# A two-block transformer on one core: order of the second block's steps around the change from grouped-query to neighbourhood attention

## Chip, cores and metric

One core of a Trainium2 chip runs the whole program. The metric is device microseconds of one execution. Three runs of the kernel before took 1642.47, 1636.21 and 1642.05 us, median 1642.05 us.

## The reference, cut to what matters

The program computes two blocks on 512 tokens of width 1024. The change lies in the second, which puts 16 meta tokens ahead of the 512 and runs two layers of this form:

```python
h = rms_norm_2(x, norm_g)
qa, ka, va, za, qb, kb, vb, zb, ga, gb = split_cols(einsum('bld,de->ble', h, w_in))
oa = gqa_attention(rope(norm(qa)), rope(norm(ka)), va) * silu(za)     # 8 heads, 2 groups
ob = neighbourhood_attention(qb, kb, vb, rpb) * silu(zb)              # 8 heads, 8x16 window and the meta keys
mixed = sigmoid(ga) * (oa @ w_o_attn) + sigmoid(gb) * (ob @ w_o_na)
return x + mixed @ w_out
```

Meta rows are queries too in the first layer; in the second they are keys only. The reference writes no order between the ten projections and the two attentions, as long as each has its inputs.

## The kernel before

Every projection is done with operands split into a high and a low part (fp32r), as three matmuls per product (`mm`, L173 to L175). A weight tile is loaded by SP (L157, 512 KB, pool `wr`, 2 buffers), its high part is cast on ACT (L137, `whi`, 3 buffers), its low part is made on GpSimd (L147, four pieces) or, in `dense` mode, on VectorE (L140).

`b2_attention` runs a layer's attention from a string of steps, `B2_ORDER[li]`. The part before the bar is grouped-query attention, the part behind it neighbourhood attention. The steps are:

- `t` rope tables, `k` keys and values, `q0` and `q1` queries of a group, each with normalisation and rope; the turned queries of `q1` go through `bankD` (L1408).
- `A hd p` scores and exponentials of two blocks of 128 queries (L1477, L1485, L1486), `P hd p` their normalisation, transposes and values (L1498, L1502, L1508, L1514, L1516), `E` the gating of a finished head, `m g` the meta queries of a group (scores L1477 with `qm`).
- `Z br pr` a gate of an attention output (L1449), `G br m` a gate of the mix (L1701): each is one weight tile and 48 matmuls of 264 columns in the first layer, 24 of 512 in the second.
- `Q pr` the neighbourhood queries and keys of two heads: two weight tiles, 96 matmuls of 264 columns in the first layer, splits, and four copies between partitions issued by SP (L1586 for the keys). `V half` the neighbourhood values: two weight tiles, 16 matmuls for the meta rows (L1348) and 96 for four tiles of tokens.
- `S hd p` neighbourhood scores (L1615, L1617, L1618, L1621), `T hd p` their normalisation and transposes (L1634, L1638, L1643), `O hd` values (L1656), `M` the meta queries.

Three facts set what a step can wait for. First, all of `Z`, `G`, `Q`, `V`, `k` and `q` take their accumulators from `bankD`: two banks of `ps_d`, and for every third call, in the order of the string, the one bank of `ps_e`:

```python
        self.nd += 1
        pool = self.ps_e if self.ps_e and self.nd % 3 == 0 else self.ps_d
```

Second, the pool `k` has 4 buffers. The two of grouped-query keys (`kd`, one a group) are free again when the last scores on them are through; each `Q` takes two (`ks`, one a head of the pair). Third, the values of neighbourhood attention (`vb`) take space of the pools `va`, `r`, `rd` and `rope`, so that they can be written only when the last values of grouped-query attention are through.

The string sets the order in which instructions are traced, not the order in which the engines get them: the tile context is opened with `schedule_with_timeline_sim=True`, which arranges each engine's queue by its own estimate of when operands are ready. Of the first steps up to three `Z` or `G` are started early: their first halves are traced one after the other, then their second halves (`early` in `b2_attention`).

Of the kernel before, what the change touches and what calls it, by code (L numbers as in the profile page):

```python
# [40 lines left out]
class Build:  # L41
# [1109 lines left out]


    B2_BANKS = dict(s=2), dict(p=1)
    B2_ORDER = ("Z01 Z00 G11 t k q0 A00 P00 Z03 A30 A01 P01 A10 E00 G03 P10 A11 P11 A20 E01 P20 A21 P21 q1 G00 A31 E02 A41 P30 A40 P31 Z02 E03 A50 A51 P40 A61 P41 E04 Z10 A60 P50 Q0 P51 G01 Q2 E05 m0 A70 A71 P60 P61 E06 G05 P70 P71 E07 G02 m1 Z11 | V0 S00 S10 S01 V1 T00 S11 T10 Q1 T11 T01 S20 O0 T20 S21 E10 O1 S30 E11 S40 S31 T21 S41 T30 O2 T40 Z12 S50 E12 T31 T41 O3 T50 E13 O4 Q3 S51 Z13 G10 S70 S60 E14 T51 G04 O5 S61 T60 E15 M S71 T61 T70 O6 G14 G13 T71 G12 E16 O7 E17", "Z00 Z02 t k q0 A00 P00 A01 P01 A10 E00 A11 P10 G11 P11 A21 A20 E01 G01 Z01 q1 P20 A40 P21 A30 E02 P30 A31 A51 P31 A41 E03 A50 P40 P41 E04 P50 P51 Z03 Z10 A60 A61 E05 Q2 A70 G10 P60 P61 E06 G00 G05 G02 Q0 P70 A71 P71 E07 | S00 V0 T00 Q1 V1 S01 S10 S11 T01 O0 S20 T10 T11 S21 E10 O1 E11 T20 T21 S40 S30 Z11 O2 E12 S31 T30 T31 S41 O3 G04 E13 T40 Z12 T41 S50 O4 T50 Q3 S51 E14 T51 O5 S60 S61 Z13 T60 S70 T61 E15 S71 G12 G14 O6 T70 E16 T71 O7 E17 G03 G13")

    def layer(self, li, h):
        nc, a = self.nc, self.a
# [31 lines left out]
    def b2_attention(self, li, h):  # L1189
# [4 lines left out]
        early = []  # L1194
        for part, pairs, pools in zip(self.B2_ORDER[li].split("|"), (True, False), (("va", "r", "rd", "rope"), ("vb",))):
            with ExitStack() as ctx:
# [636 lines left out]
```

## Time and profile before

| | us |
|---|---|
| median of 3 runs | 1642.05 |
| the profiled execution | 1641.14 |
| its span | 1639.0 |
| PE busy in the span | 1554.7 |
| DVE, ACT, POOL busy | 963.0, 765.0, 508.8 |

In the profiled execution the attention of the first layer lies at about 700 to 1060 us and that of the second at about 1195 to 1510 us. A stretch row gives, for each engine, the busy time and the number of instructions, then the granted TensorE clock, the share of DMA and the GB/s. A timeline row gives start and duration of merged instructions, what they write and read, and in brackets the idle time before them with what ended it.

### The profile page before, as it was taken

How to read it: one execution, taken by the hardware profiler on the slowest of the kernel's cores; microseconds unless marked ns; L12 is line 12 of the kernel's file. 1: busy time of each engine (PE TensorE's matmuls, PEld its weight loads, DVE VectorE, ACT ScalarE, POOL GpSimd, SP SyncE). 2: the span in 40 equal slices, each digit the busy share in tenths (PEclk: the TensorE clock that was granted, in tenths of full speed). 3: DMA queues.
4: the chain of work that ended last, by engine and by line, in shares of the span. 5: the costliest groups of instructions: out<-in, count | busy, mean ns of one | idle time of the engine just before them, and what ended most of it. 6: DMA issues, size and time to landing. Idle time of an engine off the chain costs nothing. (4 is left out here: it accounts for less than half of the span.)

```text
span 1639.0 us, 25892 instructions
## 1 busy us (share of the span) xinstructions
PE 1554.7 (95%) x9694; PEld 1378.3 (84%) x9694; DVE 963.0 (59%) x2156; ACT 765.0 (47%) x1727; POOL 508.8 (31%) x641
## 2 busy tenths in 40 slices
PE   6999999889999999999899999999999997999997
PEld 5788977778888888799898899999798896988785
DVE  4476567745444435658865558545568648665453
ACT  4465566734333323644554446433345455554332
POOL 4663443131111112325432243011455340431022
PEclk9999989989999999999998999999999999999999
DMA  5532222455333333322131134135322330342252
GB/s 163 143 112 69 65 75 82 148 185 169 90 97 96 103 104 116 104 89 78 40 87 54 54 111 131 46 92 180 116 77 78 86 92 18 99 121 88 78 183 73
DMA packets 189376, 163.60 MB, mean 100 GB/s; under 512 B 9664, under 2 KB 161312, under 8 KB 189252
## 3 DMA queue, kind: packets, MB, share of 16 engines
q1 hardware_dynamic: 189252, 161.96, 32.9%
q8 instruction: 76, 1.25, 0.3%
q14 instruction: 48, 0.39, 0.1%
HBM read 139.19 MB, written 12.58 MB: 93 GB/s over the span
## 5 line engine op out<-in xcount | busy, mean ns | idle before, releaser
L147 POOL TENSOR_TENSOR wlo<-wraw,whi 128x256 fp32r<-128x256 f32 (+1 forms) x384 | 284.3, 772 | 370.5 <-ACT whi L137 351.7
L137 ACT CAST whi<-wraw 128x1024 fp32r<-128x1024 f32 (+2 forms) x216 | 212.0, 982 | 327.8 <-PE psd L174 79.6
L173 PE MATMUL psd<-hh,whi 128*128 128x264 f32 (+2 forms) x1016 | 339.7, 335 | 3.9 <-DVE k L202 1.4
L174 PE MATMUL psd<-hl,whi 128*128 128x264 f32 (+2 forms) x1016 | 338.4, 333 | 0.0
L175 PE MATMUL psd<-hh,wlo 128*128 128x264 f32 (+2 forms) x1016 | 337.2, 332 | 0.5 <-DVE wlo L140 0.5
L140 DVE TENSOR_TENSOR wlo<-wraw,whi 128x1024 fp32r<-128x1024 f32 (+1 forms) x119 | 135.9, 1142 | 205.1 <-ACT whi L137 204.9
L173 PEld LDWEIGHTS psd<-hh,whi 128*128 128x128 f32 x1016 | 192.8, 190 | 23.1 <-ACT hh L201 1.6
L175 PEld LDWEIGHTS psd<-hh,wlo 128*128 128x128 f32 x1016 | 192.9, 190 | 18.1 <-DVE wlo L140 1.0
L174 PEld LDWEIGHTS psd<-hl,whi 128*128 128x128 f32 x1016 | 193.2, 190 | 16.9
L173 PE MATMUL psd<-whi,hh 128*128 128x256 f32 (+2 forms) x484 | 138.8, 288 | 4.9 <-ACT mo L371 2.4
L175 PE MATMUL psd<-whi,hl 128*128 128x256 f32 (+2 forms) x484 | 137.8, 285 | 0.0
L174 PE MATMUL psd<-wlo,hh 128*128 128x256 f32 (+2 forms) x484 | 137.4, 285 | 0.0
L173 PEld LDWEIGHTS psd<-whi,hh 128*128 128x128 f32 x484 | 91.5, 190 | 6.1 <-ACT mo L371 2.6
L342 POOL TENSOR_TENSOR y<-x,g 128x512 f32<-128x512 f32 (+1 forms) x34 | 46.9, 1391 | 147.3 <-DVE x L534 103.2
L201 ACT CAST pt<-pst 128x512 fp32r<-128x512 f32 (+3 forms) x130 | 63.9, 505 | 61.1 <-PE pst L1502 49.6
L175 PEld LDWEIGHTS psd<-whi,hl 128*128 128x128 f32 x484 | 91.8, 190 | 0.3
L174 PEld LDWEIGHTS psd<-wlo,hh 128*128 128x128 f32 x484 | 91.6, 190 | 0.4
L202 DVE TENSOR_TENSOR pt<-pst,pt 128x512 fp32r<-128x512 f32 (+3 forms) x130 | 75.1, 583 | 28.2 <-ACT pt L201 27.2
L1143 POOL TENSOR_TENSOR act<-conv,act 128x512 fp32r<-128x512 f32 x16 | 25.4, 1586 | 161.7 <-ACT act L1142 161.7
L1485 DVE TENSOR_REDUCE gls<-pss 128x1 f32<-128x528 f32 (+1 forms) x66 | 46.5, 704 | 38.4 <-PE pss L1477 37.5
L1486 ACT ACTIVATE pr<-pss,gls 128x528 f32<-128x528 f32 (+1 forms) x66 | 46.4, 703 | 35.2 <-DVE gls L1485 33.0
L175 PE MATMUL pss<-oh,wlo 128*128 128x264 f32 (+1 forms) x192 | 61.6, 321 | 0.0
(478 smaller groups left out, 3631.9 us busy)
## 6 DMA issues: line engine op xcount, KB each, us to landing
wraw<-in_w_in_dram SPq DMA_DIRECT2D x108, 512.0 KB
wraw<-in_w_up_dram SPq DMA_DIRECT2D x32, 512.0 KB
wraw<-in_w_out_dram SPq DMA_DIRECT2D x24, 512.0 KB
wraw<-in_w_down_dram SPq DMA_DIRECT2D x16, 512.0 KB
nbias<-in_na_bias_dram SPq DMA_DIRECT2D x16, 408.0 KB
k<-k SPq DMA_DIRECT2D x16, 296.0 KB
wraw<-in_w_ple_gate_dram SPq DMA_DIRECT2D x8, 512.0 KB
wraw<-in_w_o_attn_dram SPq DMA_DIRECT2D x16, 256.0 KB
```

The lines of the kernel that those rows point to most:

```text
L137: nc.scalar.copy(hi, raw)
L140: nc.vector.tensor_sub(lo, raw, hi.bitcast(F32))
L147: nc.gpsimd.tensor_sub(lo[:, p[0], p[1]], raw[:, p[0], p[1]], hi[:, p[0], p[1]].bitcast(F32))
L173: m(ps, A[0], B[0], start=start, stop=False)
L174: m(ps, A[0], B[1], start=False, stop=False)
L175: m(ps, A[1], B[0], start=False, stop=stop)
L201: nc.scalar.copy(hi, src)
L202: nc.vector.tensor_sub(lo, src, hi.bitcast(F32))
L342: self.nc.gpsimd.tensor_tensor(y[:n, c], x[:, c], g[:n, c], op=OP.mult)
L1143: nc.gpsimd.tensor_sub(lo, u, hi.bitcast(F32))
L1485: nc.vector.tensor_reduce(mx, sv, axis=AX.XY, op=OP.max, negate=True)
L1486: nc.scalar.activation(pr.rearrange("p (a n) -> p a n", a=2), sv, AF.Exp, bias=mx, accum_out=l)
```

## The change

The same 237 steps stand in the same four parts (two layers, ahead of the bar and behind it); only their order within a part differs.

First layer, before the bar (old above new):

```
Z01 Z00 G11 t k q0 A00 P00 Z03 A30 A01 P01 A10 E00 G03 P10 A11 P11 A20 E01 P20 A21 P21 q1 G00 A31 E02 A41 P30 A40 P31 Z02 E03 A50 A51 P40 A61 P41 E04 Z10 A60 P50 Q0 P51 G01 Q2 E05 m0 A70 A71 P60 P61 E06 G05 P70 P71 E07 G02 m1 Z11
Z01 Z00 t k q0 A00 P00 Z03 A30 G11 A01 P01 A10 E00 G03 P10 A11 P11 A20 E01 P20 A21 P21 q1 G05 A31 E02 A41 P30 G02 A40 G00 P31 Z02 E03 A50 A51 Z10 P40 A61 P41 E04 A60 P50 Q0 P51 G01 E05 m0 A70 A71 P60 P61 E06 P70 P71 Q2 E07 m1 Z11
```

Behind the bar, the first steps (the rest is as before but for S61, which goes ahead of O5):

```
V0 S00 S10 S01 V1 T00 S11 T10 Q1 T11 T01 S20 O0 T20 S21 E10 O1
V0 Q1 S00 S10 S01 T00 S11 T10 T11 T01 S20 O0 T20 S21 E10 V1 O1
```

Second layer, before the bar:

```
Z00 Z02 t k q0 A00 P00 A01 P01 A10 E00 A11 P10 G11 P11 A21 A20 E01 G01 Z01 q1 P20 A40 P21 A30 E02 P30 A31 A51 P31 A41 E03 A50 P40 P41 E04 P50 P51 Z03 Z10 A60 A61 E05 Q2 A70 G10 P60 P61 E06 G00 G05 G02 Q0 P70 A71 P71 E07
Z00 Z02 t k q0 A00 P00 A01 P01 A10 E00 A11 P10 G11 P11 A20 E01 G01 Z01 q1 A21 P20 A40 P21 A30 E02 P30 A31 A51 P31 A41 E03 A50 P40 Z10 P41 E04 P50 P51 Z03 A60 A61 E05 Q2 A70 G10 P60 P61 E06 G00 Q0 G05 P70 A71 P71 E07 G02
```

Behind its bar T10, S40 and T40 go some places forward, Z13 goes behind T60, and the gates G12 and G13 come forward from the end, to behind T30 and behind E13.

One value differs by the order: in the first layer O0 now precedes V1, whose last instruction copies the meta keys' values to partitions 32 to 47 of `vbm`; head 0 there multiplies the low parts of the meta keys' weights by what stood in those partitions.

## Rows read from the trace of the kernel before

**Rows 1.** Page, busy time of each engine over the span

```profile
PE 1554.7 (95%) x9694; PEld 1378.3 (84%) x9694; DVE 963.0 (59%) x2156; ACT 765.0 (47%) x1727; POOL 508.8 (31%) x641
```

**Rows 2.** Stretches of both layers: PE, PEld, DVE, ACT, POOL, clock, DMA share, GB/s

```profile
700.00:800.00 100.00, 93.81 (x732) 91.12 (x733) 75.70 (x193) 47.96 (x117) 48.34 (x63) 0.95 0.24 73
800.00:870.00 70.00, 70.00 (x587) 69.56 (x586) 47.66 (x100) 39.93 (x91) 22.32 (x36) 1.00 0.26 70
870.00:930.00 60.00, 52.31 (x371) 47.68 (x370) 36.38 (x77) 27.11 (x66) 11.04 (x17) 0.89 0.15 42
930.00:1060.00 130.00, 129.78 (x1103) 128.08 (x1103) 80.28 (x252) 67.59 (x172) 39.91 (x61) 1.00 0.34 99
1343.00:1393.00 50.00, 40.70 (x310) 36.15 (x309) 39.79 (x84) 27.16 (x62) 2.81 (x4) 1.00 0.13 36
```

**Rows 3.** Stretches of 10 us inside them, the same columns

```profile
780.00:790.00 10.00, 8.56 (x67) 7.26 (x66) 9.69 (x26) 7.44 (x17) 4.71 (x6) 1.00 0.01 2
790.00:800.00 10.00, 6.93 (x42) 6.51 (x42) 9.63 (x22) 3.53 (x9) 7.40 (x11) 0.83 0.37 105
...
890.00:900.00 10.00, 7.54 (x34) 6.54 (x33) 5.39 (x12) 2.66 (x9) 0.74 (x2) 0.55 0.15 31
```

**Rows 4.** Timeline of PE, first layer, around the change of attentions

```profile
884.91 0.28 PE L1516 MATMUL pso<-pm,vm 128*128 128x256 f32 x1
...
891.95 0.45 PE L1348 MATMUL psd<-whi,hm 128*48 128x256 f32 x1 [1.94 <-DVE z L1450]
...
913.50 0.73 PE L1477 MATMUL pss<-k,qm 128*64 128x264 f32 x4
...
917.65 0.39 PE L173 MATMUL psd<-hh,whi 128*128 128x264 f32 x1 [0.78 <-DVE k L202]
917.88 0.28 PE L174 MATMUL psd<-hl,whi 128*128 128x264 f32 x1
...
920.42 0.28 PE L174 MATMUL psd<-hl,whi 128*128 128x264 f32 x1
```

**Rows 5.** Timeline of ACT, first layer: key splits and gates

```profile
846.73 0.39 ACT L1701 ACTIVATE sg<-psd 128x264 f32<-128x264 f32 x1 [0.49 <-PE psd L175]
...
890.16 0.64 ACT L201 CAST k<-psd 64x264 fp32r<-64x264 f32 x2
...
914.59 0.65 ACT L201 CAST k<-psd 64x264 fp32r<-64x264 f32 x2
...
923.11 0.37 ACT L1701 ACTIVATE sg<-psd 128x264 f32<-128x264 f32 x1
```

**Rows 6.** Timeline of the SP queue, first layer: the two copies of keys

```profile
893.60 25.52 SPq L1586 DMA_DIRECT2D k<-k  x2
```

**Rows 7.** Timeline of PE, first layer, behind q1

```profile
788.17 0.66 PE L1408 MATMUL psd<-ident,rd 128*128 128x128 f32 x4 [0.84 <-DVE rd L1396]
...
794.49 0.74 PE L1514 MATMUL pso<-pt,va 128*128 128x256 f32 x4 [3.06 <-DVE pt L202]
```

**Rows 8.** Timeline of ACT, second layer: key splits of Q0

```profile
1344.66 0.37 ACT L201 CAST k<-psd 64x264 fp32r<-64x264 f32 x1
...
1383.00 0.65 ACT L201 CAST k<-psd 64x264 fp32r<-64x264 f32 x2
```

**Rows 9.** Page, group of the low parts of weights

```profile
L147 POOL TENSOR_TENSOR wlo<-wraw,whi 128x256 fp32r<-128x256 f32 (+1 forms) x384 | 284.3, 772 | 370.5 <-ACT whi L137 351.7
```

**Rows 10.** Timeline of PE, start of the first layer

```profile
711.47 0.37 PE L173 MATMUL psd<-hh,whi 128*128 128x264 f32 x1
```

**Rows 11.** Timeline of DVE, start of the first layer

```profile
712.37 0.69 DVE L202 TENSOR_TENSOR hl<-pst,hh 128x512 fp32r<-128x512 f32 x1 [0.45 <-ACT hh L201]
```

**Rows 12.** Timeline of ACT, start of the first layer

```profile
717.09 1.05 ACT L137 CAST whi<-wraw 128x1024 fp32r<-128x1024 f32 x1 [2.41 <-PE psd L174]
```

**Rows 13.** Timeline of PE, neighbourhood scores and turns of the first layer

```profile
944.50 0.40 PE L1615 MATMUL pss<-k,q 128*128 128x256 f32 x2
...
955.41 0.60 PE L1638 MATMUL pst<-ident,nsb 128*128 128x128 f32 x4
```

More of the change, by code (lines that the diff above doesn't have):

```diff
@@ L1153 @@
     B2_BANKS = dict(s=2), dict(p=1)
-    B2_ORDER = ("Z01 Z00 G11 t k q0 A00 P00 Z03 A30 A01 P01 A10 E00 G03 P10 A11 P11 A20 E01 P20 A21 P21 q1 G00 A31 E02 A41 P30 A40 P31 Z02 E03 A50 A51 P40 A61 P41 E04 Z10 A60 P50 Q0 P51 G01 Q2 E05 m0 A70 A71 P60 P61 E06 G05 P70 P71 E07 G02 m1 Z11 | V0 S00 S10 S01 V1 T00 S11 T10 Q1 T11 T01 S20 O0 T20 S21 E10 O1 S30 E11 S40 S31 T21 S41 T30 O2 T40 Z12 S50 E12 T31 T41 O3 T50 E13 O4 Q3 S51 Z13 G10 S70 S60 E14 T51 G04 O5 S61 T60 E15 M S71 T61 T70 O6 G14 G13 T71 G12 E16 O7 E17", "Z00 Z02 t k q0 A00 P00 A01 P01 A10 E00 A11 P10 G11 P11 A21 A20 E01 G01 Z01 q1 P20 A40 P21 A30 E02 P30 A31 A51 P31 A41 E03 A50 P40 P41 E04 P50 P51 Z03 Z10 A60 A61 E05 Q2 A70 G10 P60 P61 E06 G00 G05 G02 Q0 P70 A71 P71 E07 | S00 V0 T00 Q1 V1 S01 S10 S11 T01 O0 S20 T10 T11 S21 E10 O1 E11 T20 T21 S40 S30 Z11 O2 E12 S31 T30 T31 S41 O3 G04 E13 T40 Z12 T41 S50 O4 T50 Q3 S51 E14 T51 O5 S60 S61 Z13 T60 S70 T61 E15 S71 G12 G14 O6 T70 E16 T71 O7 E17 G03 G13")
+    B2_ORDER = ("Z01 Z00 t k q0 A00 P00 Z03 A30 G11 A01 P01 A10 E00 G03 P10 A11 P11 A20 E01 P20 A21 P21 q1 G05 A31 E02 A41 P30 G02 A40 G00 P31 Z02 E03 A50 A51 Z10 P40 A61 P41 E04 A60 P50 Q0 P51 G01 E05 m0 A70 A71 P60 P61 E06 P70 P71 Q2 E07 m1 Z11 | V0 Q1 S00 S10 S01 T00 S11 T10 T11 T01 S20 O0 T20 S21 E10 V1 O1 S30 E11 S40 S31 T21 S41 T30 O2 T40 Z12 S50 E12 T31 T41 O3 T50 E13 O4 Q3 S51 Z13 G10 S70 S60 E14 T51 G04 S61 O5 T60 E15 M S71 T61 T70 O6 G14 G13 T71 G12 E16 O7 E17", "Z00 Z02 t k q0 A00 P00 A01 P01 A10 E00 A11 P10 G11 P11 A20 E01 G01 Z01 q1 A21 P20 A40 P21 A30 E02 P30 A31 A51 P31 A41 E03 A50 P40 Z10 P41 E04 P50 P51 Z03 A60 A61 E05 Q2 A70 G10 P60 P61 E06 G00 Q0 G05 P70 A71 P71 E07 G02 | S00 V0 T00 Q1 V1 S01 S10 S11 T10 T01 O0 S40 S20 T11 S21 E10 O1 E11 T20 T21 S30 Z11 O2 E12 S31 T30 G12 T31 T40 S41 O3 G04 E13 G13 Z12 T41 S50 O4 T50 Q3 S51 E14 T51 O5 S60 S61 T60 Z13 S70 T61 E15 S71 G14 O6 T70 E16 T71 O7 E17 G03")
     def layer(self, li, h):
```

## The prediction

> **What bounds the kernel now.** I read the page's busy times first: PE works 1554.7 of 1639.0 us, DVE 963.0 [rows 1]. Moving steps takes no matmul away, so only the 84 us in which PE stands idle, and the time in which it runs slowly, can be won or added to. The stretches then say where this lies in the code that is moved [rows 2]. From 800 to 870 PE is busy for all of the 70.00 us, and in the neighbourhood attention from 930 to 1060 for 129.78 of 130. It is not full in three places: 700 to 800 (idle 6.2 us), 870 to 930 (idle 7.7 us, with a mean clock of 0.89) and 1343 to 1393 (idle 9.3 us, clock 1.00).
>
> The ten-microsecond stretches and the timelines say why. **At the first layer's change** no engine is full: from 890 to 900 DVE is busy 5.39 us, ACT 2.66, and the clock is granted at 0.55, between the two levels of 1.2 and 2.4 GHz, after PE's gap of 1.94 us [rows 3, 4]. What is missing is a place to write. Q2's keys lie in two of the three banks of `bankD`; their split for one head is made at 890.16, for the other only at 914.59, 24.4 us later [rows 5], since that head's buffer is the grouped-query key `kd[1]`, and its last readers are the meta scores of m1 at 913.50 [rows 4]. Only then, at 917.65, released by the split of `k`, does the next half gate begin on PE; its tanh follows at 923.11 [rows 4, 5]. SP stands behind the same wait: its two copies of keys take from 893.60 to 919.12 [rows 6].
>
> **Behind q1** (780 to 800) DVE is busy 9.69 and 9.63 of 10 us [rows 3], and PE waits for the rope of a turn that itself sits in a bank of `bankD` and, for 3.06 us, for a split [rows 7]. I take the stall as 1.4 + 3.1 us idle plus 17% of 6.93 us for the clock of 0.83: 5.7 us. That at 870 to 930 is 7.7 us plus 11% of 52.31 us: 13.5 us.
>
> **In the second layer** all gates have run early, Q0 holds two banks from about 1344.66 until `kd[1]` comes free and the split at 1383.00 can be made [rows 8], and PE gets little but grouped-query work. DVE is busy 39.79 of 50 us there [rows 2].
>
> Two things follow. A gate is not done where it stands in the string: G01 stands behind P51, but its first tanh is through at 846.73 and P51's last matmul only at 884.91 [rows 4, 5], since the build arranges each queue by estimate. And what counts of an order is which work is left when grouped-query attention runs dry, and which banks it finds.
>
> **The change, part by part.** A gate or Z issues one load on SP, one cast on ACT, four GpSimd pieces of 0.77 us [rows 9] and 48 matmuls; 21 starts from 917.88 to 920.42 give 0.121 us each [rows 4], so 5.8 us of PE. Q and V issue two loads, casts and eight pieces, and 11 to 14 us of PE. All of it is issued in both orders; what is moved is the cover.
>
> *Start, first layer.* G11 is no longer the third early step. Its first half runs on PE from 711.47, while the low part of the last token tile is not there before 712.37 + 0.69 = 713.06 [rows 10, 11]: 1.6 us without cover now. Against it, the first key weights find a free `whi` buffer, where their cast at 717.09 had waited 2.41 us for PE to finish with one [rows 12]. Bounds 0 to +2.9 (a whole half); I take **+1.6**. SP passes one load fewer before the rope tables' loads.
>
> *G11 ahead of A01.* Its 5.8 us of PE now lie between q0 and q1, and grouped-query attention starts that much earlier. The stall behind q1 is 5.7 us, of which DVE's share moves forward with the start. But its other half is banks: the turns of q1 keep their three, and G05 behind them takes the place of G00. Bounds -5.7 to 0; I take **-4**.
>
> *G05, G02 and Z10 early, Q2 late.* By the count of `bankD` calls, G02's first half and Z11's second half fell on the banks that Q2's keys held. Now 96 matmuls (11.6 us) come ahead of Q2, so its hold begins later, while m1, which ends it, keeps its place; and behind Q2 only Z11 follows, with one half on a held bank. G02's half (24 x 0.121 = 2.9 us) is then not left over, and with it one `whi` buffer fewer is held, so that the second weights of V0 can be cast and one tile of V0 can run in the stall, another 2.9 us. Of the 13.5 us I take **-5**, by the two halves, less a little since the fillers also run out earlier; bounds -13.5 (the hold is gone) to +3 (one half more is shut in).
>
> *Q1 ahead of S00, V1 behind E10.* Q1 goes past the bias loads in SP's queue, and its eight GpSimd pieces past V1's; GpSimd is busy 39.91 of 130 us there [rows 2]. Its keys need the buffers of heads 0 and 1, whose last scores (S11) now stand behind it, so it holds two banks until then. The trace has no such hold here; its cover is V0 and the first half of Q1, and the scores wait for T00, which before came 10.9 us behind S01 only because V1 was on PE [rows 13]. Bounds 0 to +10 (the hold of 24.4 us at the rate of the first layer's, 13.5 us lost in 60, is 5.5 us; twice that with copies and biases behind it on SP); I take **+1**, nearest to the full stretch of 930 to 1060.
>
> *Second layer.* G02 behind E07 is the only gate left for the dry end; Q0, two gates ahead, takes one bank of each kind, so G05, G02 and one tile of V0 share the third. But V0's meta rows, which had the `ps_e` bank, now wait. A21 leaves DVE to q1. Bounds -5.8 to +5.8 (one gate under the stall, or one more shut out); I take **0**. G12, G13, T10, S40, T40 and S61 move within full PE time and cost nothing while it is full; if that cover went, each gate would cost up to its four pieces, 3.1 us.
>
> Sum: 1.6 - 4 - 5 + 1 + 0 = -6.4 us. Against the profiled execution's 1641.1 us, 0.9 us under the median of 1642.05, this gives 1634.7, said as 1635.
>
> **A rule against it.** The second layer's gaps repeat for 40 us while DVE is not full [rows 2]. The Trainium skill (Perfetto Trace Analysis, Optimization Strategy) says that the same gap repeating on the engine that should be full can mean too little SBUF or PSUM for the next tile. The trace agrees for the 24.4 us between the two splits; by that rule alone an order that leaves buffers and banks as they are leaves the stall, as in the second rival.
>
> **The rivals.**
> 1. *The hold goes over to Q1* (slower). If the build puts Q1's keys on PE ahead of T00 and S11, two banks are shut where PE was full. For it: four buffers in `k` and ten tiles that ask for them, and the picture of 890 to 917. Against: DVE and ACT have room, and T00 needs 0.6 us of PE. It decides if Q1's key matmuls end over 10 us before S11's scores. Price +10, with +1.6 at the start and nothing won: 1653.
> 2. *Nothing moves* (no change). Queues are arranged by estimate, so the gates run in whatever gaps there are, and the keys still wait for m1. G11's start loss and gain cancel: 1641.
> 3. *Both dry ends fill* (much faster). G02 of the second layer runs in its stall (-5.8), Q2 comes so late that its hold falls under m1 (-10), the clock stays up, q1 gives 5: 1641.1 + 1.6 - 5 - 10 - 5.8 = 1622.
>
> **How the numbers follow.** A measurement of this kernel tells about 0.5%, 8.2 us, from no change. The forecast has 0.42; its own range is 1628 to 1641, about half of it beyond 0.5% (0.20 faster, 0.22 same). Rival 3 has 0.22, all faster: the rows show 28.5 us to be had. Rival 2 has 0.14, same. Rival 1 has 0.22, nearly all slower (0.20, and 0.02 same). Faster 0.42, same 0.38, slower 0.20. The range goes into both outer rivals, to 1619 and 1653, and leaves some 0.1 out on either side.
>
> **What would show it.** Right: idle time of PE at 780 to 800 down to 2 us; between Q2's two key splits clearly under 24.4 us, or a gate and a V0 tile on PE between them; the clock nearer 1.00 there; the neighbourhood stretch still full. Wrong: a new gap on PE between V0 and T00 with a key split of Q1 as its end (rival 1), or the same two stalls with the same releasers (rival 2).

## The result, and the profile after

The changed kernel takes 1628.88 us, the median of six runs (1626.32 to 1632.74), against 1641.39 us for six runs of the kernel before: a ratio of 0.9933 with a 95% interval of 0.9919 to 0.9948. It is about 12 us faster where 6.4 were forecast. Its profiled execution took 1628.86 us.

The busy times of the page after, and the stretches that answer to [rows 1 to 3], with the same columns:

```profile
PE 1547.4 (95%) x9694; PEld 1372.4 (84%) x9694; DVE 959.1 (59%) x2156; ACT 765.1 (47%) x1727; POOL 506.3 (31%) x641
```

```profile
700.00:800.00 100.00, 93.72 (x753) 91.55 (x753) 79.67 (x196) 50.63 (x123) 50.46 (x66) 0.96 0.23 67
780.00:790.00 10.00, 8.77 (x76) 8.51 (x76) 9.63 (x24) 5.97 (x16) 2.70 (x3) 1.00 0.01 2
790.00:800.00 10.00, 6.39 (x36) 5.37 (x36) 9.65 (x21) 6.06 (x13) 8.82 (x12) 0.74 0.29 84
...
870.00:930.00 60.00, 57.45 (x470) 55.23 (x470) 37.06 (x98) 30.70 (x74) 15.95 (x26) 1.00 0.25 71
890.00:900.00 10.00, 9.77 (x79) 9.00 (x79) 6.78 (x19) 5.43 (x14) 1.60 (x4) 1.00 0.33 85
930.00:1060.00 130.00, 128.18 (x1082) 126.26 (x1081) 80.08 (x237) 67.69 (x169) 35.02 (x55) 1.00 0.33 94
1343.00:1393.00 50.00, 44.33 (x323) 40.34 (x322) 35.46 (x82) 26.96 (x64) 8.71 (x12) 0.97 0.17 50
```

The number of instructions is the same on every engine, and DVE, ACT and POOL work as long as before to within 4 us. PE's busy time is 7.3 us lower for the same 9694 matmuls; fewer of them fall into stretches of a lower granted clock. The place is the first layer's change: from 890 to 900 PE now does 79 matmuls in 9.77 us at clock 1.00, where it did 34 in 7.54 us at 0.55 [rows 3], and 870 to 930 holds 470 matmuls instead of 371 [rows 2]. Behind q1 (780 to 800) nothing is better: 15.16 us of 20 busy against 15.49, and the clock of the second ten is lower than before.

**A ledger of the stalls.** To say where the time came from I add up, over PE's matmuls, the interval from one start to the next less the median interval of that line and shape in the kernel before. It is the time lost to gaps and to the lower clock alike:

| stretch | before, us | after, us | difference | the prediction's term |
|---|---|---|---|---|
| start of the first layer, 640 to 760 | 10.9 | 10.5 | -0.4 | +1.6 |
| around q1, 760 to 830 | 9.0 | 8.4 | -0.6 | -4 |
| 830 to the second of Q2's two key splits | 13.4 | 1.6 | **-11.8** | -5 |
| from there through the neighbourhood part | 6.8 | 9.0 | +2.2 | +1 |
| second layer, up to 1540 | 27.1 | 26.7 | -0.4 | 0 |

The sum is -11.0 us, and the span is 11.9 us shorter (1627.1 against 1639.0); the first projection of the layer began 1.5 us sooner (699.20 against 700.75), which no step of the change can have done, so a microsecond or two of a single profiled execution is chance.

**The stretch between the two splits is as long as it was.** I call it the hold, as the prediction does. The timeline of ACT after, key splits of Q2 (those of [rows 5]), then that of PE at the end of the hold (as in [rows 4]):

```profile
883.48 0.38 ACT L201 CAST k<-psd 64x264 fp32r<-64x264 f32 x1
...
888.43 0.37 ACT L201 CAST k<-psd 64x264 fp32r<-64x264 f32 x1
...
907.73 0.66 ACT L201 CAST k<-psd 64x264 fp32r<-64x264 f32 x2
```

```profile
904.96 0.39 PE L1508 MATMUL pst<-ident,pr 128*16 128x128 f32 x2 [0.23 <-DVE pt L202]
906.17 0.66 PE L1502 MATMUL pst<-ident,pr 128*128 128x128 f32 x4 [0.83 <-DVE pt L202]
...
910.80 0.39 PE L173 MATMUL psd<-whi,hh 128*128 128x256 f32 x1 [0.79 <-DVE k L202]
```

From the first split to the last it is 24.25 us, before 24.43, and it ends by the same releaser, the split of `k` on DVE. The banks themselves are shut from an earlier time on, since the keys are written before they are split. Counted back in halves of 24 matmuls from the gates that follow, the last matmul of Q2's keys is, first in the kernel before, then after:

```profile
869.07 0.37 PE L175 MATMUL psd<-hh,wlo 128*128 128x264 f32 x1
```

```profile
887.15 0.28 PE L175 MATMUL psd<-hh,wlo 128*128 128x264 f32 x1
```

So both banks are shut for 45 us before (869.44 to 914.59) and for 20 us after (887.43 to 907.73): the hold of the banks does begin later, as the prediction had it. Before, the first split waited in this time until m0's scores at 889.30 were done with its buffer. What also changed is what lies between the splits. PE's groups between the two splits, first the kernel before (890.16 to 914.59), then after (883.48 to 907.73); the columns are matmul, tiles, shapes and count, busy time and mean ns of one, and the idle time before them:

```profile
L1514 PE MATMUL pso<-pt,va 128*128 128x32 f32 x16 | 3.8, 375 | 0.2 <-ACT pt L201 0.2
...
L1348 PE MATMUL psd<-whi,hm 128*48 128x256 f32 x4 | 1.7, 426 | 1.9 <-DVE z L1450 1.9
L1348 PE MATMUL psd<-wlo,hm 128*48 128x256 f32 x4 | 1.7, 418 | 0.0
```

```profile
L174 PE MATMUL psd<-hl,whi 128*128 128x264 f32 x16 | 4.6, 290 | 0.0
L173 PE MATMUL psd<-hh,whi 128*128 128x264 f32 x16 | 4.6, 290 | 0.0
L175 PE MATMUL psd<-hh,wlo 128*128 128x264 f32 x16 | 4.6, 284 | 0.0
...
L173 PE MATMUL psd<-whi,hh 128*128 128x256 f32 x8 | 2.3, 292 | 0.0
L175 PE MATMUL psd<-whi,hl 128*128 128x256 f32 x8 | 2.3, 290 | 0.0
L174 PE MATMUL psd<-wlo,hh 128*128 128x256 f32 x8 | 2.2, 281 | 0.0
L1514 PE MATMUL pso<-pt,va 128*128 128x32 f32 x16 | 2.0, 257 | 0.0
L1348 PE MATMUL psd<-wlo,hm 128*48 128x256 f32 x8 | 2.0, 283 | 0.0
L1348 PE MATMUL psd<-whi,hm 128*48 128x256 f32 x8 | 2.0, 282 | 0.0
```

I call the matmuls of L173 to L175 and L1348 fillers, since none of them waits for the grouped-query chain. Before there were 8 in the hold, after there are 88: two halves of 24 with 264 columns, one tile of V0 (24 with 256) and 16 for the meta rows. One of the halves is the second half of Q2's own first head, whose split follows at 888.43. The 16 small value matmuls (L1514, 128x32), which both kernels have there, show the clock: 375 ns each before, 257 after.

### The profile page after: what moved, and what is told of

It is laid out like the page before. It is cut to its first block, busy times and chain, and to the rows that moved or that the text cites. A ratio compares the mean times of both kernels' runs of the same rounds, so it can differ in the third digit from the quotient of the medians.

```text
span 1627.1 us, 25892 instructions
## 1 busy us (share of the span) xinstructions
PE 1547.4 (95%) x9694; PEld 1372.4 (84%) x9694; DVE 959.1 (59%) x2156; ACT 765.1 (47%) x1727; POOL 506.3 (31%) x641
## 4 chain that ended last, share of the span: by engine, by line
PE 75%; DVE 9%; DMA 6%; ACT 5%; issue 2%; POOL 2%; SPq 0%; POOLq 0%; ACTq 0%; DVEq 0%
PE psd L173 14%; PE psd L174 13%; PE psd L175 13%; PE pss L173 7%; PE pss L174 7%; PE pss L175 7%; PE pso L1514 2%; PE pss L1477 2%; ACT whi L137 2%; PE pst L1502 1%; DMA wraw<-in_w_in_dram 1%; POOL wlo L147 1%; PE pss L1615 1%; DMA wraw<-in_w_out_dram 1%; PE pso L1656 1%
## 5 line engine op out<-in xcount | busy, mean ns | idle before, releaser
L173 PE MATMUL psd<-hh,whi 128*128 128x264 f32 (+2 forms) x1016 | 339.4, 335 | 2.6 <-ACT hh L201 1.1
L175 PE MATMUL psd<-hh,wlo 128*128 128x264 f32 (+2 forms) x1016 | 337.5, 333 | 0.0
L173 PEld LDWEIGHTS psd<-hh,whi 128*128 128x128 f32 x1016 | 192.9, 190 | 21.8 <-ACT hh L201 1.6
L175 PEld LDWEIGHTS psd<-hh,wlo 128*128 128x128 f32 x1016 | 193.1, 190 | 17.3 <-DVE wlo L140 0.3
L173 PE MATMUL psd<-whi,hh 128*128 128x256 f32 (+2 forms) x484 | 138.7, 288 | 5.0 <-ACT mo L371 2.2
L175 PE MATMUL psd<-whi,hl 128*128 128x256 f32 (+2 forms) x484 | 137.4, 284 | 0.0
L173 PEld LDWEIGHTS psd<-whi,hh 128*128 128x128 f32 x484 | 90.9, 188 | 7.3 <-ACT mo L371 2.5
L175 PEld LDWEIGHTS psd<-whi,hl 128*128 128x128 f32 x484 | 91.1, 188 | 0.3
L175 PE MATMUL pss<-oh,wlo 128*128 128x264 f32 (+1 forms) x192 | 61.6, 321 | 0.0
```

The lines of the kernel that those rows point to most:

```text
L173: m(ps, A[0], B[0], start=start, stop=False)
L175: m(ps, A[1], B[0], start=False, stop=stop)
```

## The experiments

All ratios are against the kernel before on the same chip, five rounds each.

### Which of the first layer's moves carries it

**q2_late.** The kernel before with Q2 alone moved:

```diff
- P50 Q0 P51 G01 Q2 E05 m0 A70 A71 P60 P61 E06 G05 P70 P71 E07 G02 m1 Z11
+ P50 Q0 P51 G01 E05 m0 A70 A71 P60 P61 E06 G05 P70 P71 Q2 E07 G02 m1 Z11
```

> The kernel before with one step moved: Q2 of the first layer goes from behind G01 to behind P71; all else as before. In both kernels 24 us pass between Q2's two key splits; what differs is how many matmuls PE finds for that time (8 before, 86 after). Theory: Q2's place alone leaves that work over, so this kernel takes 9 to 12 us less than before, some 1630, with the clock near 1.00 between the key splits. Rival: the gates G05, G02 and Z10 going early, or G11's move, are needed as well, and Q2's move alone gives under 4 us (1637 or more).

Measured: 1637.34 us (12 runs), ratio 0.9981 (0.9966 to 0.9995). Its splits are at 889.34 and 914.82, and from 890 to 900 the clock is as low as before:

```profile
890.00:900.00 10.00, 8.63 (x39) 8.13 (x40) 4.86 (x12) 2.04 (x6) 0.74 (x2) 0.52 0.14 31
```

The theory fell, and the rival's 1637 us or more held. By its runs Q2's place is worth 1 to 6 us; in its trace, of an execution near the slowest of the twelve (1641.92), the stall is all there (13.5 us in the ledger).

**q2_back.** The changed kernel with Q2 in its old place:

```diff
- P50 Q0 P51 G01 E05 m0 A70 A71 P60 P61 E06 P70 P71 Q2 E07 m1 Z11
+ P50 Q0 P51 G01 Q2 E05 m0 A70 A71 P60 P61 E06 P70 P71 E07 m1 Z11
```

> The changed kernel with Q2 of the first layer put back behind G01; all else as changed. Theory: the work for the time between the key splits is used up early again, PE's clock falls there, and the time goes up by 8 to 11 us over the changed kernel, to about 1638. Rival (the other moves carry the gain): it stays within 3 us of the changed kernel, about 1629 to 1632.

Measured: 1631.68 us, ratio 0.9941 (0.9922 to 0.9960), inside the interval of the change, as the rival had it. That Q2's late place carries the gain fell.

**g11.** The kernel before with G11 alone moved:

```diff
- Z01 Z00 G11 t k q0 A00 P00 Z03 A30 A01 P01
+ Z01 Z00 t k q0 A00 P00 Z03 A30 G11 A01 P01
```

> The kernel before with one step moved: G11 of the first layer goes from the third place to behind A30. Theory (the turns of q1 keep the banks, so that a gate more ahead of them does not reach the stall behind q1): within 2 us of before, 1639 to 1643, the stretch from 780 to 800 still losing 6 us or more. Rival (the prediction's term): 2 to 4 us faster, with the stall behind q1 halved.

Measured: 1631.64 us, ratio 0.9940 (0.9919 to 0.9962). This one move gives nearly all of it, more than the theory (within 2 us) or the rival (2 to 4 us) allowed. And it gives it where the change does: the stall behind q1 stays (8.6 us for 760 to 830, before 9.0), that from 830 to the second split falls from 13.4 to 4.3 us. Timelines of ACT and DVE in this kernel around Q2's first key split:

```profile
881.73 0.38 ACT L1701 ACTIVATE sg<-psd 128x264 f32<-128x264 f32 x1
...
882.01 0.63 ACT L201 CAST k<-psd 64x264 fp32r<-64x264 f32 x2
...
885.40 0.39 ACT L1701 ACTIVATE sg<-psd 128x264 f32<-128x264 f32 x1 [1.97 <-PE psd L175]
```

```profile
893.81 0.42 DVE L1450 SCALAR_TENSOR_TENSOR z<-z,psd 128x264 f32<-128x264 f32 x1
```

and the same in the kernel before, whose first split is in [rows 5] at 890.16:

```profile
878.98 0.39 ACT L1701 ACTIVATE sg<-psd 128x264 f32<-128x264 f32 x1
...
882.64 0.39 ACT L1701 ACTIVATE sg<-psd 128x264 f32<-128x264 f32 x1 [1.68 <-PE psd L175]
```

```profile
891.46 0.43 DVE L1450 SCALAR_TENSOR_TENSOR z<-z,psd 128x264 f32<-128x264 f32 x1
```

The last three fillers are the same in both, by the string a half of G05, one of G02 and one of Z11, and run 2.3 to 2.8 us later than before. The chain of grouped-query attention runs 8 us sooner (split 882.01 against 890.16; first score 746.51 against 754.15), of which 5.8 us are the gate's 48 matmuls that no longer stand ahead of the keys. So the halves of G02 and Z11 slid from before the split to behind it, where PE had nothing else: 48 of the 56 fillers that this kernel has there. In both kernels the same fillers run while both banks are shut, four halves and 8 matmuls of V0's meta rows; only their place against the chain differs.

**after_old_na.** The changed kernel with the old first layer behind the bar (V1 ahead of T00, Q1 behind T10, S61 behind O5):

```diff
- | V0 Q1 S00 S10 S01 T00 S11 T10 T11 T01 S20 O0 T20 S21 E10 V1 O1
+ | V0 S00 S10 S01 V1 T00 S11 T10 Q1 T11 T01 S20 O0 T20 S21 E10 O1
```

> The changed kernel with the first layer's steps behind the bar in the order of before (V1 ahead of T00, Q1 behind T10). Theory: the 1.5 us gap and the other loss that the changed kernel shows between V0 and S11 are the price of Q1 ahead of S00, so this kernel takes 2 to 3 us less than the changed one, about 1626. Rival: those gaps are there for another reason (the earlier end of grouped-query attention), and the time stays within 1 us of the changed kernel.

Measured: 1631.38 us, ratio 0.9936 (0.9913 to 0.9960). The time doesn't tell the two orders apart. The trace does, a little: PE is busy for all 130.00 us from 930 to 1060, against 128.18 after, and the ledger has 6.7 us for the neighbourhood part against 9.0. The changed order's loss is here, in the timeline of PE after:

```profile
945.14 0.38 PE L173 MATMUL psd<-whi,hh 128*128 128x256 f32 x1 [0.44 <-DVE pmeta L168]
...
954.02 0.50 PE L1615 MATMUL pss<-k,q 128*128 128x256 f32 x2 [1.38 <-DVE nst L1618]
```

PE waits for a scores bank, not for Q1's keys.

### Why the place of one gate counts

Two theories were left, named A and B in what follows: that a filler taken from the head is then left over for the dry end (A), or that the keys and queries starting earlier is itself the gain (B).

**g11_across.** G11 leaves the grouped-query part:

```diff
- Z01 Z00 G11 t k q0 | V0 S00 S10 S01 V1 T00 S11 T10 Q1
+ Z01 Z00 t k q0 | V0 S00 S10 S01 V1 T00 S11 T10 G11 Q1
```

> The kernel before with one step moved: G11 of the first layer goes from the head of the grouped-query part to behind the bar, just ahead of Q1. Theory A (a filler taken from the head counts because more fillers are then left over for the dry end under Q2's two key splits): here the filler leaves the grouped-query part altogether, so the head gets shorter but nothing is added under the hold, and PE does the gate's 5.8 us later in a stretch that is full: the time stays within 3 us of the kernel before. Theory B (the earlier start of the keys and queries is itself the gain, with no filler needed at the dry end): the same gain as when G11 went to behind A30, 10 to 12 us under the kernel before. Signs: matmuls on PE between Q2's two key splits (8 before, 86 after the change) stay near 8 by B with the gain there all the same; by A they grow only where the gain does.

Measured: 1638.88 us, ratio 0.9985 (0.9973 to 0.9997). The first score, at 748.75, is 5.4 us sooner than before (7.6 with g11), and the time is within 2 or 3 us of the kernel before. B falls. The last grouped-query values are 7.1 us sooner, and 4.2 of these are paid back in the neighbourhood part, which was full.

**z00.** Z00 moved instead of G11:

```diff
- Z01 Z00 G11 t k q0 A00 P00 Z03 A30 A01
+ Z01 G11 t k q0 A00 P00 Z03 A30 Z00 A01
```

> The kernel before with Z00 of the first layer, instead of G11, moved from the head to behind A30; G11 stays early. Theory A and theory B both: any step of 48 matmuls taken from the head gives what G11 gave, 9 to 12 us under the kernel before (ratio near 0.994). Rival C: the gain is particular to G11 (its bank by the count of three, or that it is a gate with no reader in this layer's attention), then Z00 gives under 4 us.

Measured: 1636.58 us, ratio 0.9969 (0.9954 to 0.9984): half of what G11 gives, between the two expectations. 33 fillers lie in the hold.

**g11_last.** G11 at the very end of the grouped-query part:

```diff
- E07 G02 m1 Z11 |
+ E07 G02 m1 Z11 G11 |
```

> The kernel before with G11 of the first layer moved from the head to the end of the grouped-query part, behind Z11. Theory A: the filler goes straight to the dry end, so the same gain as behind A30, 8 to 13 us under the kernel before, with at least 40 more matmuls between Q2's two key splits. Rival C': so late it finds the banks shut by Q2's keys and runs only behind the second split, so the stretch 870 to 930 keeps its idle time, and the gain is under 6 us.

Measured: 1638.50 us, ratio 0.9982 (0.9969 to 0.9995). The rival C' is right in the time, and in PE's idle time from 870 to 930 (7.8 us, before 7.7); the clock is 1.00 there all the same. 25 fillers lie in the hold; by the count of banks below, 24 of them are one half of G11 (tanh at 889.15), and its other half comes behind the second split.

**g11_twice.** G11 done at the head and again behind A30, 48 matmuls of added work:

```diff
- Z01 Z00 G11 t k q0 A00 P00 Z03 A30 A01
+ Z01 Z00 G11 t k q0 A00 P00 Z03 A30 G11 A01
-        th = self.sg[br, m] = self.T(pool, [128, L2])
+        if (br, m) not in self.sg:
+            self.sg[br, m] = self.T(pool, [128, L2])
+        th = self.sg[br, m]
```

> The kernel before with G11 of the first layer done twice: at the head as before, and once more behind A30 (the same gate written again, so 48 matmuls more on PE, 5.8 us). Theory A (fillers pushed back into the dry end are the gain): the stall from 830 us to Q2's second key split, 13 us before and 4 us with G11 moved, falls to about 4 to 6 us although nothing is taken from the head, with some 40 to 60 matmuls in the hold; so 8 us won, 5.8 us paid, and the time is 1 to 5 us under the kernel before in spite of the added work. Theory B (the earlier start of the keys and queries is the gain): nothing is won and the work is paid, 4 to 7 us over the kernel before.

Measured: 1649.91 us, ratio 1.0053 (1.0032 to 1.0074), 8.6 us slower. Both theories missed the time, and A fell in the form in which I had put it: a filler more in the string is not a filler at the dry end. There is none at all in this kernel's hold, and the longest wait of the series. Its timeline of PE:

```profile
892.60 0.69 PE L1477 MATMUL pss<-k,qm 128*64 128x264 f32 x4 [0.72 <-ACT pr L1486]
897.12 1.25 PE L1477 MATMUL pss<-k,q 128*128 128x264 f32 x4 [3.83 <-ACT pr L1486]
```

Its timeline of ACT around the splits of Q2's keys (L1703 is the L1701 of the other kernels):

```profile
885.67 0.38 ACT L1703 ACTIVATE sg<-psd 128x264 f32<-128x264 f32 x1
...
893.18 0.39 ACT L1703 ACTIVATE sg<-psd 128x264 f32<-128x264 f32 x1
893.46 0.64 ACT L201 CAST k<-psd 64x264 fp32r<-64x264 f32 x2
...
917.98 0.65 ACT L201 CAST k<-psd 64x264 fp32r<-64x264 f32 x2
...
925.10 0.38 ACT L1703 ACTIVATE sg<-psd 128x264 f32<-128x264 f32 x1
928.60 0.38 ACT L1703 ACTIVATE sg<-psd 128x264 f32<-128x264 f32 x1
```

Only two halves of gates run between the end of Q2's key matmuls and the last split, where before three run and one of Z11. The banks account for it. In the string, the added gate is two more calls of `bankD` ahead of Q2, so that by the count of three Q2's keys take both banks of `ps_d`, where they took one of `ps_d` and the one of `ps_e` before. Then only calls of `ps_e` find a bank: by the count a half of G05 (885.67) and one of G02 (893.18); their other halves are the tanhs at 925.10 and 928.60. So this run changes the banks along with the work and is no clean test of an added filler; one with the count kept was not made.

**g11_z00.** Both fillers moved:

```diff
- Z01 Z00 G11 t k q0 A00 P00 Z03 A30 A01
+ Z01 t k q0 A00 P00 Z03 A30 G11 Z00 A01
```

> The kernel before with both G11 and Z00 of the first layer moved from the head to behind A30. Theory A: the stall of 13 us can be filled only once; with G11 alone some 4 us of it were left, so the second filler adds at most 4 us: 10 to 15 us under the kernel before, like the changed kernel. Theory B: the start of the keys comes another 10 us sooner, so 18 us or more under the kernel before.

Measured: 1634.06 us, ratio 0.9953 (0.9936 to 0.9969), no more than G11 alone and below A's 10 to 15 us; B's 18 us are far off. The hold has the same 56 fillers as g11; the stretch around q1 lost 10.9 us in the ledger instead of 8.6.

**What the series shows.** The hold has the same grouped-query work in every kernel, to within three transposes. Its length less 0.121 us [rows 4] for each filler in it is what that work and its waits took:

| kernel | hold, us | fillers in it | less fillers, us | lowest clock in a 5 us slice | ratio |
|---|---|---|---|---|---|
| g11_twice | 24.52 | 0 | 24.5 | 0.50 | 1.0053 |
| q2_late | 25.48 | 12 | 24.0 | 0.50 | 0.9981 |
| l1_only | 24.60 | 8 | 23.6 | 0.50 | 0.9990 |
| before | 24.43 | 8 | 23.5 | 0.50 | |
| g11_across | 20.02 | 9 | 18.9 | 0.70 | 0.9985 |
| g11_last | 20.52 | 25 | 17.5 | 1.00 | 0.9982 |
| z00 | 21.10 | 33 | 17.1 | 1.00 | 0.9969 |
| g11 | 22.24 | 56 | 15.5 | 1.00 | 0.9940 |
| q2_back | 22.09 | 59 | 15.0 | 1.00 | 0.9941 |
| after | 24.25 | 88 | 13.6 | 1.00 | 0.9933 |

The more fillers the build puts between the two splits, the less of the chain's own waits is left on the path, down to 13.6 us. (g11_z00 has the row of g11, the other kernels with the changed first layer that of after.) The ratios follow, but for kernels that paid elsewhere: g11_across does G11 in the neighbourhood part, g11_last does half of it behind the splits, and g11_twice does it twice. Each row is one execution; those of z00 (1631.53 us), g11_last (1634.61) and l1_only (1636.08) were among their fastest, those of q2_late and g11_twice (1653.86) among their slowest.

**Which fillers can run.** The count of `bankD` calls fits the first layer of every trace here. One number in it is free, where the count starts; it is set by the kernel before, where a half of G02 and one of Z11 are left over behind the last split (tanh at 923.11 in [rows 5], Z11's at 929.55). In q2_late, too, Q2's keys take both banks of `ps_d`, since G05 went ahead of Q2, so that run does not test Q2's place alone. In every other kernel they take one bank of each pool.

### The second layer

**l1_only.** The kernel before with the changed order of the second layer.

```diff
- A61 E05 Q2 A70 G10 P60 P61 E06 G00 G05 G02 Q0 P70 A71 P71 E07 |
+ A61 E05 Q2 A70 G10 P60 P61 E06 G00 Q0 G05 P70 A71 P71 E07 G02 |
```

> The kernel before with the second layer's order of the changed kernel alone. The trace of the changed kernel has the same stalls in the second layer as before (26.7 against 27.1 us over the median pitch of PE), so this should be within 3 us of the kernel before. If it is over 5 us faster, part of the gain is the second layer's and the sum of the first layer's is too large.

Measured: 1639.56 us, ratio 0.9990 (0.9977 to 1.0003). No part of the gain can be told to be its own.

**after_fill.** The changed kernel with two gates more ahead of the second layer's bar; they are taken from behind it, where they stood behind T30 and O3:

```diff
- P70 A71 P71 E07 G02 |
+ P70 A71 P71 E07 G02 G12 G04 |
```

> The changed kernel with two gates of the second layer, G12 and G04, moved from behind the bar to the end of the grouped-query part, behind G02. Theory A carried to the second layer, whose dry end of some 14 us the change left as it was: two more gates of 24 matmuls are to be had there, so 5 to 10 us under the changed kernel, a ratio to the kernel before of 0.987 to 0.990. Rival D: Q0's keys hold the banks of that end, the two gates run ahead of it or behind it and the neighbourhood part has less to fill with: within 2 us of the changed kernel.

Measured: 1644.32 us, ratio 1.0021 (1.0010 to 1.0033), so 14 us worse than the changed kernel. No tanh falls between 1341.11 and 1380.09, and Q0's last key split is at 1369.48: its keys hold the banks, and the two gates come behind them, as rival D has it, though at 14 us and not its 2. The neighbourhood part then runs dry at its end (15.8 us in the ledger from 1488 to 1533, 1.7 in the changed kernel). Stretches of this kernel, then its timeline of PE:

```profile
1393.00:1500.00 107.00, 106.81 (x674) 94.96 (x673) 58.31 (x175) 51.04 (x121) 32.14 (x45) 1.00 0.36 103
1500.00:1530.00 30.00, 22.23 (x104) 17.96 (x104) 19.52 (x49) 15.49 (x36) 0.00 (x0) 0.79 0.13 41
```

```profile
1508.30 0.77 PE L1615 MATMUL pss<-k,q 128*128 128x256 f32 x2 [3.41 <-DVE nst L1618]
...
1522.00 0.51 PE L1651 MATMUL pso<-pm,vm 128*128 128x512 f32 x1 [1.95 <-DVE pm L202]
...
1524.90 0.77 PE L173 MATMUL pss<-oh,whi 128*128 128x512 f32 x1 [1.49 <-DVE corr L1461]
```

**after_mix.** The old first layer behind the bar, and Q0 of the second at the end of its part:

```diff
- E06 G00 Q0 G05 P70 A71 P71 E07 G02 |
+ E06 G00 G05 P70 A71 P71 E07 Q0 G02 |
```

> The changed kernel with the old order of the first layer behind the bar, and in the second layer Q0 moved to the end of the grouped-query part, behind E07 (ahead of G02). Theory A carried on: in the second layer Q0's keys shut two banks for some 50 us; with Q0 late its own 100 or so matmuls are the filler for the dry end and the hold is short, so the stall there falls from 14 us by 5 to 8 us: 1622 to 1627 us. Rival D: the gates run earlier instead and the dry end keeps its size, or the neighbourhood part runs dry at its end, as when two gates were taken from it: 1629 us or more.

Measured: 1629.73 us, ratio 0.9934 (0.9915 to 0.9954), the same as the changed kernel. Q0's first key split is at 1321.70 and the last at 1368.82; in the changed kernel they are at 1318.97 and 1368.79. The hold is 2.7 us shorter, and a gate that ran in it (tanh at 1342.80 in the changed kernel) now runs ahead of it (1310.69), as rival D has it; the stall of the second layer's dry end stays at 14 to 15 us. No version here beats the changed kernel by what can be told.

## Why the prediction was right, and which steps were not

The direction held and the time lies in the range (1635 forecast, range 1619 to 1653, measured 1628.88), though the gain is twice the forecast one, and two of the signs named for the forecast were there: **a tile of V0 and half of a gate on PE between Q2's two key splits, and the clock at 1.00 there**. The sum came out at half because its terms were shared out wrongly; that it came out no worse is luck in part, since what the term of G11 lacked in its own place it gave in another's.

*Start, +1.6.* Nothing was lost: -0.4 us in the ledger, and the first score is 8.1 us sooner, 5.8 of them the gate itself.

*G11 ahead of A01, -4.* This is the step that failed, in its place. The prediction let G11's 5.8 us fall into the stall behind q1. Its sign, idle time at 780 to 800 down to 2 us, is missing: 4.84 us are idle, before 4.51 [rows 3]. The stall stayed in the change and in g11, where the ledger has -0.6 and -0.4 us, and DVE is busy 9.63 and 9.65 of 10 us there, as before [rows 3]. The move is worth 10 us all the same, 100 us further on: it shifts the chain forward against the fillers, and the last of them fall into the hold.

*G05, G02 and Z10 early, Q2 late, -5.* The place was right, the term mis-sized: from 830 to the second split 11.8 us were won. So was the prediction's picture of it, one tile of V0 and halves not left over. But most of its cause was not this step's: g11 reaches -9.1 us there (13.4 to 4.3) without Q2 or any of the three gates moved. The later start of the banks' hold is real, 20 us of shut banks where there were 45 and where g11 still has 33, but what is left for it and the three gates is the 2.7 us between 4.3 and 1.6, which the times of g11 and the changed kernel don't tell apart. The three gates were not tried without G11.

*What was left out of the sum.* The term priced the idle time and the clock of [rows 2] together and took two fifths. The two go together: g11_across has one filler more in its hold than the kernel before and is 4.6 us shorter net of fillers, though PE's idle time between the splits is much the same (4.5 us against 5.0, from the groups). What differs is PE's busy time for the same chain, with the clock, which falls to 0.70 for one slice instead of 0.50 and 0.53 for two. In the kernels below g11_across in the table it stays at 1.00, and these some 4 us are back as a whole.

*Q1 and V1, +1.* The ledger has +2.2 us, by a wait for scores banks; the run can't tell it from nothing. The first rival's mechanism, Q1's keys holding two banks, is not in the trace: no gap of PE between V0 and T00 ends with a split of Q1.

*Second layer, 0.* Confirmed by l1_only. The stall there stayed with its cause, Q0's hold, from the first head's second key split to the last 47.5 us long now (1321.33 to 1368.79) against 38.3 [rows 8].

*The rule against it.* The Trainium skill (Perfetto Trace Analysis, Optimization Strategy) reads a repeating gap on the engine that should be full as a sign that SBUF or PSUM may be short. In the first layer the trace agrees that banks are short, with two of three shut for 45 us. What I drew from it, that an order which leaves buffers and banks as they are leaves the stall, fails: the stall went from 13.4 to 1.6 us by order alone, in g11 to 4.3 with the banks still shut for 33. In the second layer no order tried moved it, and there the trace agrees; more key buffers were not tried.

*What stays open.* Which fillers find a bank can be read off the string by the count of calls, but not how many of them the build puts into the hold: z00 gets 33 where g11 gets 56 with the same banks. I had theory A say that a filler saved is a filler at the dry end; the runs allow only that the place of the head's gate against the chain can put it there. The experiments show that the stall follows the fillers in the hold, not why the build arranges them so.

## What to carry to other kernels

Look for a stall's cure on the path ahead of it: a step of fill-in work that stands in front of a long chain delays the chain by its whole length and is missing at the chain's dry end. Moving it behind the chain's start won 10 us, some 100 us further on, while moving it to the end of the chain or past it won 2 to 3 us. An added gate lost 9 us: it also changed which banks the next keys took, so count the banks of the steps behind a moved one. Where a tool arranges the queues, count in the trace what lies in the dry stretch, for the order that is written says little about it. And take fill-in work only from a stretch that has some to spare: two gates taken from the second layer's full neighbourhood part cost 14 us.

## What was not expected of the hardware

How much of a short stall is clock. In the kernel before PE had waits of 0.72 and 1.94 us around m0's scores (the second is in [rows 4]); from 895 to 900 the clock stood at 0.50, which is the lower level of 1.2 GHz, with PE busy 4.75 of 5 us, and it was back at 1.00 from 905:

```profile
890.00:895.00 5.00, 2.79 (x13) 2.28 (x12) 4.04 (x9) 1.79 (x6) 0.53 (x1) 0.61 0.07 17
895.00:900.00 5.00, 4.75 (x23) 4.26 (x22) 1.35 (x3) 0.87 (x3) 0.21 (x1) 0.50 0.22 45
```

In g11_across waits of 1.35 and 1.58 us stand 5 us apart, with work at full speed between them, and the clock fell to 0.70 in one slice only:

```profile
885.00:890.00 5.00, 3.07 (x25) 2.57 (x23) 3.58 (x10) 2.17 (x8) 0.53 (x1) 1.00 0.65 167
890.00:895.00 5.00, 4.33 (x34) 3.77 (x35) 3.07 (x12) 2.46 (x7) 0.21 (x1) 0.96 0.01 3
895.00:900.00 5.00, 4.69 (x26) 4.17 (x25) 3.88 (x8) 2.05 (x5) 0.00 (x0) 0.70 0.00 0
```

In g11_last PE is busy only 3.42 to 4.89 of every 5 us from 875 to 905, with waits of up to 1.58 us, and the clock is 1.00 in all of these slices. By the table, the chain took 23.5 to 24.5 us where the clock fell to 0.50 and 18.9 where it fell to 0.70 for one slice. Between the kernel before and g11_across 0.5 us of this is idle time, so some 4 us go with the clock. That it was these waits that brought the clock down is read from their order in time; no run varied them alone.
